# Whole-head scores in PSUM for the attention's softmax, and the pool mixer's window sums moved behind the state recurrence

## The chip, the cores and the metric

The kernel runs on one core of a Trainium2 chip. The metric is the device time of one execution in microseconds (us), taken as the median of several runs. TensorE (PE) does matmuls and writes to PSUM, VectorE (DVE) and ScalarE (ACT) read PSUM and do elementwise work and reductions, GpSimd (POOL) works in SBUF alone, and SyncE (SP) issues most transfers. Each engine runs its own instructions in order; engines wait for each other through semaphores.

## The reference, cut to what matters

Two transformer-like blocks follow each other on 1024 tokens of width 1024. The first has a bidirectional state-space mixer beside an attention, then a mixture of experts; the second has a pool mixer beside a state-space mixer, then a gated feed-forward network. The change touches two pieces.

```python
# first block, attention: 16 query heads on 4 key heads, 64 wide, 1024 queries, 256 + 1024 keys
s = jnp.einsum('bqhgd,bkhd->bhgqk', q_blk, k) * scale
pr = jax.nn.softmax(s, axis=-1)
o = jnp.einsum('bhgqk,bkhd->bqhgd', pr, v)
...
# second block: u = rmsnorm(h) @ w_in, one half to each mixer
for gi, w in enumerate((2, 4, 8, 16)):            # pool mixer, 128 channels per window
    mean = (c - lagged) / jnp.minimum(n_pos, float(w))
    diffs.append(mean - ug[:, :, gi])
y_pool = einsum('blgc,gcd->blgd', stack(diffs), w_pool) * pool_scale
...
y = gelu(state-space output)                      # state-space mixer: recurrence, then a gate
y = y * jax.nn.sigmoid(y @ w_glu + b_glu)
h = h + concatenate([y_pool, y_ssm]) @ w_out
```

## The kernel before

Products of fp32 values are made from a high and a low part, so a matrix product in `mm3` (lines 213 to 217) is three matmuls, and many tensors are split into a cast (ACT) and the rest (DVE or POOL).

**Attention** (`attention`, from line 1099). For each of 8 blocks of 128 queries and each of 4 key heads there is a group of 4 query heads, so 32 groups. A group's heads come as two pairs, and the work of a pair is cut into five *products* of at most 512 score columns: a head has T = 1280 of them (`PIECES`). The body of the loop over `s` (lines 1231 to 1246) is one *step*. It issues, in this order: `products(n)`, which are two accumulated matmuls of 512 columns, or four of 256 in the middle step of a pair; `maxima` of an earlier product on DVE; the `transposes` of the probabilities of four heads for one of the ten blocks of 128 keys (four matmuls into `pt`); `low`, the low part of an earlier transposed block (DVE); `exps`, the exponentials of a product (ACT), whose bias is the negated maximum and which add up their row sums; `norms`, the reciprocal of a sum (DVE) and the scaling of the probabilities (POOL); `high`, the cast of the transposed block (ACT); and `values`, two matmuls with the values into `pv`. At the end of a group `evacuate` copies `pv` out in two halves (ACT, lines 1223 and 1224) and POOL adds them. This order is written out by hand (`manual_schedule`), products run AHEAD = 17 steps before the values that use them.

Each product has a score tile of its own, one PSUM bank `S0` to `S4` with one buffer, so a bank is free for its next product five steps later, when its exponentials have read it. `pt` has two buffers and `pv` one. A head's maximum is made of three partial ones (`mx`), its sum of three partial sums on POOL (lines 1174 and 1175). The probabilities of a head stand in two tiles, `P0` (512 columns) and `P1` (768).

**Mixers of the second block** (`mixers`, from line 2115). TensorE projects while DVE runs the recurrence of states (`step`, `starts`, `combine`, lines 2199 to 2232), which fills `E`. Then come `out_ssm(q)` for four quarters (products with `E`, gelu on ACT), `turned(c)` (transposes, copies and a split of the gelu's output, its low part on DVE in line 2317), and the gate: eight products of twelve matmuls, each with a tanh (ACT) and a multiplication (DVE, line 2345). The generator `windows()` yields pieces of the window sums (DVE, lines 2253 to 2278): six are taken ahead of the gate, and the others two by two between its products; `pool_out(g)` (six matmuls, two evacuations on ACT) follows at three places between them and once at the end. The order on PE, DVE and POOL is written out by hand here too; ACT is left to the scheduler. The next stage (`out2`) multiplies all channels `yc` with `w_out`.

Of the kernel before, what the change touches and what calls it, by code (L numbers as in the profile page):

```python
# [10 lines left out]
F = mybir.dt.float32  # L11
# [154 lines left out]
class Kernel:  # L166
# [936 lines left out]
    def attention(self):  # L1103
# [6 lines left out]
        with es:  # L1110
# [6 lines left out]
            PIECES = (((0, 0, 512),), ((0, 512, 1024),), ((0, 1024, 1280), (1, 1024, 1280)), ((1, 0, 512),), ((1, 512, 1024),))  # L1117
            AHEAD = 17
            NG = 4 * NB
            P, split, pvs, bank = {}, {}, {}, {}  # L1120
            mx, neg, tot, rt = {}, {}, {}, {}

            def products(n):
# [7 lines left out]
                S = bank[n] = pp.tile([128, 512], F, name=f"S{k}")  # L1131
                o = 0
                for e, a, z in PIECES[k]:
                    for m in range(2):
                        nc.tensor.matmul(S[:, o:o + z - a], qS[b][:, 4 * j + 2 * p + e, :], kS[4 * m + j][:, a:z], start=m == 0, stop=m == 1)  # L1135
                    o += z - a

            def maxima(n):
                pair, k = divmod(n, 5)
                if n < 0 or pair >= 2 * NG:  # L1140
                    return
                if k == 0:
                    mx[pair] = wp.tile([128, 2, 3], F, name="mx")
                m = mx[pair]
                if k == 2:
                    V.tensor_reduce(m[:, :, 2], bank[n].rearrange("p (e n) -> p e n", e=2), axis=AX.X, op=OP.max)
                else:
                    V.tensor_reduce(m[:, k // 3, k % 3:k % 3 + 1], bank[n], axis=AX.X, op=OP.max)  # L1148
                if k in (2, 4):
                    e = k // 2 - 1  # L1150
                    h = 2 * pair + e

                    hd = wp.tile([128, 8], F, name="hd", bufs=6)
                    neg[h], tot[h], rt[h] = hd[:, 0:1], hd[:, 1:4], hd[:, 4:6]
                    V.tensor_reduce(neg[h], m[:, e, :], axis=AX.X, op=OP.max, negate=True)  # L1155

            def exps(n):

                pair, k = divmod(n, 5)
                if n < 0 or pair >= 2 * NG:  # L1160
                    return
                o = 0
                for e, a, z in PIECES[k]:
                    h = 2 * pair + e
                    half = int(a > 0)
                    if (h, half) not in P:
                        P[h, half] = wp.tile([128, 768 if half else 512], F, name=f"P{half}", bufs=9 if half else 6)
                    i = k - 2 * e
                    x = P[h, half][:, a - 512 * half:z - 512 * half]
                    nc.scalar.activation(x, bank[n][:, o:o + z - a], AF.Exp, bias=neg[h], accum_out=tot[h][:, i:i + 1])  # L1170
                    o += z - a
                    if k == 2 + 2 * e:
                        r = rt[h]
                        nc.gpsimd.tensor_add(r[:, 0:1], tot[h][:, 0:1], tot[h][:, 1:2])
                        nc.gpsimd.tensor_add(r[:, 1:2], r[:, 0:1], tot[h][:, 2:3])

            def norms(n):
                pair, k = divmod(n, 5)
                if n < 0 or pair >= 2 * NG or k not in (2, 4):
                    return  # L1180
                h = 2 * pair + k // 2 - 1
                r = rt[h]
                V.reciprocal(r[:, 0:1], r[:, 1:2])  # L1183
                for half in range(2):
                    nc.gpsimd.tensor_scalar(P[h, half], P[h, half], r[:, 0:1], 1.0, op0=OP.mult, op1=OP.mult)  # L1185
# [1526 lines left out]
```

## Time and profile before

| what | value |
|---|---|
| median of 3 runs (lowest, highest) | 2743.65 us (2742.18, 2745.04) |
| the profiled execution's own time | 2740.33 us |
| its span, first to last instruction | 2738.4 us |
| busy: PE, DVE, ACT, POOL | 2536.7 (93%), 1951.2 (71%), 1336.1 (49%), 976.5 (36%) us |
| mean granted TensorE clock | 0.959 of full speed |
| chain that ended last, by engine | PE 64%, DVE 16%, ACT 7%, DMA 6%, issue 5%, POOL 2% |
| attention, first to last score product | 800.3 to 1267.9 us |
| pool windows, their first and last shared additions (line 2264) | 1927.6 to 1952.6 us |

The page gives shares over the whole span, but the program is a row of stages with limits of their own. What a change of one stage is worth is read from that stage: from the busy time of its engines in windows of time, from what each engine waited for there, and from the timeline, where each row has a start, a duration and, in brackets, the idle time just before it and what ended it. A merged row ("x2") shows the time from the first start to the last end, and ends of matmuls are modelled, so the distance between starts tells more than their durations. The clock column says what share of the full 2.4 GHz TensorE was granted.

### The profile page before, as it was taken

The numbers are of one execution on the slowest core, as the hardware profiler recorded it, in microseconds if no ns is written. First come the engines' busy times: TensorE is split into PE (matmuls) and PEld (weight loads), VectorE is DVE, ScalarE is ACT, GpSimd is POOL, SyncE is SP. The second block draws the span as 40 slices with busy tenths as digits, with TensorE's granted clock in tenths as the row PEclk, the third lists the DMA queues.
The fourth block names the chain that finished last, engine by engine and source line by source line (L and its number), as shares of the span: only waits on it lengthen the run. The fifth ranks groups of instructions, "written<-read, shape, count | busy, mean of one in ns | idle before, by whom it ended". The sixth has DMA issues, their size and how long they took to land.

```text
span 2738.4 us, 36247 instructions
## 1 busy us (share of the span) xinstructions
PE 2536.7 (93%) x12369; PEld 2000.4 (73%) x12369; DVE 1951.2 (71%) x3735; ACT 1336.1 (49%) x2788; POOL 976.5 (36%) x1128
## 2 busy tenths in 40 slices
PE   7899999998899999998997999689799999999898
PEld 4676778854677777776775777577577788887787
DVE  7655676689649898897566777675647878775755
ACT  3233453456529999998223455343444333333433
POOL 5612011166016666666334455100241345443000
PEclk9999999988999999999987999899899999999999
DMA  7556421000610000002317788631312445547653
GB/s 270 175 189 204 155 71 39 32 8 1 245 62 17 17 17 32 17 1 69 116 70 221 223 263 264 215 109 46 112 54 74 164 148 184 173 159 269 232 196 116
DMA packets 141113, 344.21 MB, mean 126 GB/s; under 512 B 21200, under 2 KB 41344, under 8 KB 132064
## 3 DMA queue, kind: packets, MB, share of 16 engines
q1 hardware_dynamic: 88752, 198.03, 21.0%
q0 software_dynamic: 24176, 102.39, 11.5%
q10 hardware_dynamic: 28000, 41.46, 4.4%
q8 instruction: 98, 1.61, 0.2%
q14 instruction: 87, 0.71, 0.1%
HBM read 257.64 MB, written 93.62 MB: 128 GB/s over the span
## 4 chain that ended last, share of the span: by engine, by line
PE 64%; DVE 16%; ACT 7%; DMA 6%; issue 5%; POOL 2%; SPq 0%; ACTq 0%; DVEq 0%; POOLq 0%
PE m L217 5%; PE mm L215 5%; PE m L215 5%; PE m L216 5%; PE mm L217 5%; PE mm L216 5%; PE S L1135 5%; PE pt L1194 4%; PE a L216 3%; PE a L217 3%; PE a L215 2%; ACT P L1170 2%; PE pv L1215 2%; PE pv L1216 2%; PE cv L216 2%
## 5 line engine op out<-in xcount | busy, mean ns | idle before, releaser
L1203 DVE TENSOR_TENSOR pl<-pt,ph 128x512 fp32r<-128x512 f32 x320 | 219.1, 685 | 51.7 <-ACT ph L1199 46.3
L1170 ACT ACTIVATE P<-S,hd 128x512 f32<-128x512 f32 (+1 forms) x384 | 238.0, 624 | 1.8 <-DVE hd L1155 1.8
L1185 POOL TENSOR_SCALAR P<-P,hd 128x512 f32<-128x512 f32 (+1 forms) x256 | 202.7, 805 | 90.1 <-DVE hd L1183 85.5
L1135 PE MATMUL S<-kS,qS 128*128 128x512 f32 (+1 forms) x768 | 210.9, 372 | 19.1 <-ACT P L1170 19.1
L1199 ACT CAST ph<-pt 128x512 fp32r<-128x512 f32 x320 | 187.7, 587 | 28.0 <-PE pt L1194 14.5
L1194 PE MATMUL pt<-consts,P 128*128 128x128 f32 x1280 | 193.5, 273 | 6.0 <-DVE pl L1203 4.9
L1194 PEld LDWEIGHTS pt<-consts,P 128*128 128x128 f32 x1280 | 156.6, 140 | 45.2 <-DVE pl L1203 8.9
L1148 DVE TENSOR_REDUCE mx<-S 128x1 f32<-128x512 f32 x256 | 173.6, 679 | 3.0 <-PE S L1135 2.2
L1135 PEld LDWEIGHTS S<-kS,qS 128*128 128x128 f32 x768 | 128.3, 190 | 63.9 <-ACT P L1170 42.9
L1215 PE MATMUL pv<-ph,vS 128*128 128x512 f32 x320 | 151.3, 473 | 0.9 <-ACT ph L1199 0.3
L600 DVE SCALAR_TENSOR_TENSOR acc<-cv,vcol,acc 128x254 f32<-128x254 f32 (+5 forms) x288 | 110.3, 432 | 51.6 <-ACT acc L602 49.2
L2632 ACT CAST oh<-st 128x1024 fp32r<-128x1024 f32 x77 | 80.5, 1053 | 109.8 <-PE a L217 41.9
L216 PE MATMUL a<-ol,oh 128*128 128x512 f32 x308 | 122.0, 396 | 10.9 <-DVE ol L2633 10.9
L2633 DVE TENSOR_TENSOR ol<-st,oh 128x1024 fp32r<-128x1024 f32 x77 | 93.4, 1235 | 52.0 <-ACT oh L2632 45.1
L1216 PE MATMUL pv<-pl,vS 128*128 128x512 f32 x320 | 126.8, 396 | 0.2 <-DVE pl L1203 0.2
L217 PE MATMUL a<-oh,ol 128*128 128x512 f32 x308 | 121.7, 395 | 0.0
L215 PE MATMUL a<-oh 128*128 128x512 f32 x308 | 117.3, 391 | 0.3 <-DVE u L2550 0.3
L2440 ACT CAST gh<-gst 128x512 fp32r<-128x512 f32 x88 | 54.6, 621 | 128.1 <-PE m L216 122.0
L216 PE MATMUL mm<-wl,hH 128*128 128x512 f32 x288 | 114.6, 398 | 2.2 <-DVE wl L255 2.0
L215 PE MATMUL mm<-wh,hH 128*128 128x512 f32 x288 | 115.4, 401 | 0.0
L217 PE MATMUL mm<-wh,hL 128*128 128x512 f32 x288 | 113.5, 394 | 0.0
L217 PE MATMUL cv<-hH,wl 128*128 128x512 f32 (+1 forms) x288 | 104.0, 361 | 1.0 <-POOL wl L584 1.0
(785 smaller groups left out, 7494.5 us busy)
## 6 DMA issues: line engine op xcount, KB each, us to landing
gst<-in_ffn_gu_dram SPq DMA_DIRECT2D x88, 256.0 KB, 3.3
st<-hop SPq DMA_DIRECT2D x77, 256.0 KB, 7.4
wmod<-in_w_mod_dram ACTq DMA_DIRECT2D x64, 256.0 KB, 4.0
hop<-h POOLq DMA_DIRECT2D x44, 256.0 KB, 2.6
d<-in_ffn_down_dram SPq DMA_DIRECT2D x22, 512.0 KB, 3.5
wop<-d POOLq DMA_DIRECT2D x22, 512.0 KB, 3.5
st<-wop SPq DMA_DIRECT2D x44, 256.0 KB, 5.0
wst<-in_w_in_dram SPq DMA_DIRECT2D x40, 256.0 KB, 3.6
```

The source lines that it names most:

```text
L215: nc.tensor.matmul(out, lh, rh, start=first, stop=False)
L216: nc.tensor.matmul(out, lh, rl, start=False, stop=False)
L217: nc.tensor.matmul(out, ll, rh, start=False, stop=last)
L1135: nc.tensor.matmul(S[:, o:o + z - a], qS[b][:, 4 * j + 2 * p + e, :], kS[4 * m + j][:, a:z], start=m == 0, stop=m == 1)
L1148: V.tensor_reduce(m[:, k // 3, k % 3:k % 3 + 1], bank[n], axis=AX.X, op=OP.max)
L1170: nc.scalar.activation(x, bank[n][:, o:o + z - a], AF.Exp, bias=neg[h], accum_out=tot[h][:, i:i + 1])
L1185: nc.gpsimd.tensor_scalar(P[h, half], P[h, half], r[:, 0:1], 1.0, op0=OP.mult, op1=OP.mult)
L1194: nc.tensor.transpose(pt[:, i, :], P[4 * g + i, int(c > 3)][:, o:o + 128], self.ident)
L1199: nc.scalar.copy(split[n][1], split[n][0])
L1203: V.tensor_sub(split[n][2], split[n][0], split[n][1])
L1215: nc.tensor.matmul(pv, v, ph, start=c == 0, stop=False)
L1216: nc.tensor.matmul(pv, v, pl, start=False, stop=c == NBT - 1)
```

## The change

In the attention the five score tiles become one tile `S` of two whole heads, 2 x 1280 columns without a gap, over five banks; the middle bank holds the end of the first head and the start of the second. The pieces of the second head are cut anew (0 to 256, 256 to 768, 768 to 1280). A head gets one maximum, one exponential with one sum, one reciprocal and one scaling, all over 1280 columns, once its last product is issued (`head(n)` says when). The partial maxima, the POOL additions of sums and the two-part probabilities go. The exponentials stand two steps behind the products where it was four, the norms three where it was five, and AHEAD is 16. In the mixer, `window(3 - q)` is no generator any more and is issued whole, behind `out_ssm(q)`; `pool_out` follows one quarter later, `turned(0)` as before behind the third quarter, and the gate's loop holds nothing else.

```diff
@@ -1114,11 +1114,11 @@
             vS = cp.tile([128, NBT, 512], R, name="vS")
             nc.sync.dma_start(vS[:].bitcast(F), self.vv[:].rearrange("b p n -> p b n").bitcast(F))
 
-            PIECES = (((0, 0, 512),), ((0, 512, 1024),), ((0, 1024, 1280), (1, 1024, 1280)), ((1, 0, 512),), ((1, 512, 1024),))
-            AHEAD = 17
+            PIECES = (((0, 0, 512),), ((0, 512, 1024),), ((0, 1024, 1280), (1, 0, 256)), ((1, 256, 768),), ((1, 768, 1280),))
+            S = pp.tile([128, 2, T], F, name="S")
+            AHEAD = 16
             NG = 4 * NB
-            P, split, pvs, bank = {}, {}, {}, {}
-            mx, neg, tot, rt = {}, {}, {}, {}
+            P, split, pvs, cols = {}, {}, {}, {}
 
             def products(n):
 
@@ -1128,70 +1128,41 @@
                     return
                 if n % 40 == 30 and b + 1 < NB:
                     self.load_q(b + 1)
-                S = bank[n] = pp.tile([128, 512], F, name=f"S{k}")
-                o = 0
                 for e, a, z in PIECES[k]:
                     for m in range(2):
-                        nc.tensor.matmul(S[:, o:o + z - a], qS[b][:, 4 * j + 2 * p + e, :], kS[4 * m + j][:, a:z], start=m == 0, stop=m == 1)
-                    o += z - a
+                        nc.tensor.matmul(S[:, e, a:z], qS[b][:, 4 * j + 2 * p + e, :], kS[4 * m + j][:, a:z], start=m == 0, stop=m == 1)
+
+            def head(n):
+
+                pair, k = divmod(n, 5)
+                return None if n < 0 or pair >= 2 * NG or k not in (2, 4) else 2 * pair + k // 2 - 1
 
             def maxima(n):
-                pair, k = divmod(n, 5)
-                if n < 0 or pair >= 2 * NG:
-                    return
-                if k == 0:
-                    mx[pair] = wp.tile([128, 2, 3], F, name="mx")
-                m = mx[pair]
-                if k == 2:
-                    V.tensor_reduce(m[:, :, 2], bank[n].rearrange("p (e n) -> p e n", e=2), axis=AX.X, op=OP.max)
-                else:
-                    V.tensor_reduce(m[:, k // 3, k % 3:k % 3 + 1], bank[n], axis=AX.X, op=OP.max)
-                if k in (2, 4):
-                    e = k // 2 - 1
-                    h = 2 * pair + e
-
-                    hd = wp.tile([128, 8], F, name="hd", bufs=6)
-                    neg[h], tot[h], rt[h] = hd[:, 0:1], hd[:, 1:4], hd[:, 4:6]
-                    V.tensor_reduce(neg[h], m[:, e, :], axis=AX.X, op=OP.max, negate=True)
+                h = head(n)
+                if h is not None:
+
+                    cols[h] = wp.tile([128, 8], F, name="hd", bufs=6)
+                    V.tensor_reduce(cols[h][:, 0:1], S[:, h % 2], axis=AX.X, op=OP.max, negate=True)
 
             def exps(n):
-
-                pair, k = divmod(n, 5)
-                if n < 0 or pair >= 2 * NG:
-                    return
-                o = 0
-                for e, a, z in PIECES[k]:
-                    h = 2 * pair + e
-                    half = int(a > 0)
-                    if (h, half) not in P:
-                        P[h, half] = wp.tile([128, 768 if half else 512], F, name=f"P{half}", bufs=9 if half else 6)
-                    i = k - 2 * e
-                    x = P[h, half][:, a - 512 * half:z - 512 * half]
-                    nc.scalar.activation(x, bank[n][:, o:o + z - a], AF.Exp, bias=neg[h], accum_out=tot[h][:, i:i + 1])
-                    o += z - a
-                    if k == 2 + 2 * e:
-                        r = rt[h]
-                        nc.gpsimd.tensor_add(r[:, 0:1], tot[h][:, 0:1], tot[h][:, 1:2])
-                        nc.gpsimd.tensor_add(r[:, 1:2], r[:, 0:1], tot[h][:, 2:3])
+                h = head(n)
+                if h is not None:
+                    P[h] = wp.tile([128, T], F, name="P", bufs=8)
+                    nc.scalar.activation(P[h], S[:, h % 2], AF.Exp, bias=cols[h][:, 0:1], accum_out=cols[h][:, 1:2])
 
             def norms(n):
-                pair, k = divmod(n, 5)
-                if n < 0 or pair >= 2 * NG or k not in (2, 4):
-                    return
-                h = 2 * pair + k // 2 - 1
-                r = rt[h]
-                V.reciprocal(r[:, 0:1], r[:, 1:2])
-                for half in range(2):
-                    nc.gpsimd.tensor_scalar(P[h, half], P[h, half], r[:, 0:1], 1.0, op0=OP.mult, op1=OP.mult)
+                h = head(n)
+                if h is not None:
+                    V.reciprocal(cols[h][:, 2:3], cols[h][:, 1:2])
+                    nc.gpsimd.tensor_scalar(P[h], P[h], cols[h][:, 2:3], 1.0, op0=OP.mult, op1=OP.mult)
 
             def transposes(n):
                 g, c = divmod(n, NBT)
                 if n < 0 or g >= NG:
                     return
                 pt = pp.tile([128, 4, 128], F, name="pt", bufs=2)
-                o = 128 * (c - 4 if c > 3 else c)
                 for i in range(4):
-                    nc.tensor.transpose(pt[:, i, :], P[4 * g + i, int(c > 3)][:, o:o + 128], self.ident)
+                    nc.tensor.transpose(pt[:, i, :], P[4 * g + i][:, 128 * c:128 * c + 128], self.ident)
                 split[n] = pt, wp.tile([128, 4, 128], R, name="ph", bufs=4), wp.tile([128, 4, 128], R, name="pl", bufs=4)
 
             def high(n):
@@ -1236,10 +1207,10 @@
                     maxima(n - 1)
                     transposes(s + 2)
                     low(s + 1)
-                    exps(n - 4)
+                    exps(n - 2)
                     if last:
                         evacuate(s)
-                    norms(n - 5)
+                    norms(n - 3)
                     high(s + 2)
                     if not last:
                         values(s)
@@ -2266,24 +2237,17 @@
                         V.tensor_add(nx[:, 17:], u[:, 1:], u[:, 0:L - 1])
                         V.tensor_copy(nx[:, 16:17], u[:, 0:1])
                     cur = nx
-                    yield
                 t16 = pw.tile([128, 16], F, name="t16")
                 V.tensor_mul(t16, cur[:, 16:32], rc[:, 16 * g:16 * g + 16])
                 d = cur[:, 16:]
                 V.scalar_tensor_tensor(d, d, 1.0 / (2 << g), u, op0=OP.mult, op1=OP.subtract)
                 V.tensor_sub(d[:, 0:16], t16, u[:, 0:16])
-                yield
                 dh, dl = pw.tile([128, L], R, name="dh"), pw.tile([128, L], R, name="dl")
                 nc.scalar.copy(dh, d)
                 V.tensor_sub(dl, d, dh)
                 outs[g] = dh, dl
-                yield
 
             outs = {}
-
-            def windows():
-                for g in (3, 2, 1, 0):
-                    yield from window(g)
 
             def pool_out(g):
                 dh, dl = outs[g]
@@ -2322,16 +2286,17 @@
             V.tensor_scalar(hb, vc[:, off["b_glu"][0]:off["b_glu"][0] + 4], 0.5, None, op0=OP.mult)
             for q in range(4):
                 out_ssm(q)
-                if q > 1:
-                    turned(q - 2)
+                window(3 - q)
                 if q == 2:
-                    V.tensor_sub(wgl, wg, wgh)
+                    turned(0)
+                if q:
+                    pool_out(4 - q)
+            V.tensor_sub(wgl, wg, wgh)
+            turned(1)
+            pool_out(0)
             turned(2)
             turned(3)
             self.dump("Y", Y)
-            win = windows()
-            for _ in range(6):
-                next(win)
             for c in range(4):
                 for n in range(2):
                     s = slice(512 * n, 512 * n + 512)
@@ -2343,14 +2308,6 @@
                     nc.scalar.activation(th, ps, AF.Tanh, bias=hb[:, c:c + 1])
                     y = self.yc[:, 4 + c, s]
                     V.scalar_tensor_tensor(y, th, 1.0, y, op0=OP.add, op1=OP.mult)
-                    if c or n:
-                        for _ in range(2):
-                            next(win, None)
-                    if (c, n) in ((1, 1), (2, 1), (3, 1)):
-                        pool_out(4 - c)
-            for _ in win:
-                pass
-            pool_out(0)
             man.close()
             self.dump("yc", self.yc)
         s_es.close()
```

The built program shows what that makes of each engine's instructions; a bracket names the semaphores (by engine) that an instruction waits for.

TensorE in the attention before, from the last matmul of one product over three steps (`S_7989` and the like are the banks of their products; further transposes of a step are left out):

```order
L1135 MATMUL S_7989<-kS_6346,qS 128x512
L1194 MATMUL pt<-consts,P_7664 128x128 [waits DVE_49]
L1215 MATMUL pv<-ph,vS 128x512
L1216 MATMUL pv<-pl,vS 128x512
L1135 MATMUL S_8010<-kS_6342,qS 128x256 [waits Activation_49]
L1135 MATMUL S_8010<-kS_6346,qS 128x256
L1194 MATMUL pt<-consts,P_7664 128x128 [waits DVE_49]
L1215 MATMUL pv<-ph,vS 128x512
L1216 MATMUL pv<-pl,vS 128x512
L1135 MATMUL S_8032<-kS_6342,qS 128x512 [waits Activation_49]
L1135 MATMUL S_8032<-kS_6346,qS 128x512
```

and with the change, over as much of the program, from the fourth product of a pair (`S` is the one tile; `kS_6343` and the like are keys of key heads; behind the first step the transposes and values are left out):

```order
L1133 MATMUL S<-kS_6343,qS 128x512
L1133 MATMUL S<-kS_6347,qS 128x512
L1165 MATMUL pt<-consts,P 128x128 [waits DVE_49]
L1186 MATMUL pv<-ph,vS 128x512 [waits Activation_49]
L1187 MATMUL pv<-pl,vS 128x512
L1133 MATMUL S<-kS_6343,qS 128x512 [waits DVE_49]
L1133 MATMUL S<-kS_6347,qS 128x512
L1133 MATMUL S<-kS_6344,qS 128x512 [waits Activation_49]
L1133 MATMUL S<-kS_6348,qS 128x512
L1133 MATMUL S<-kS_6344,qS 128x512 [waits DVE_49]
L1133 MATMUL S<-kS_6348,qS 128x512
L1133 MATMUL S<-kS_6344,qS 128x256 [waits Activation_49]
```

Before, each product waits for ACT. Now the fourth product of a pair waits for nothing, the fifth for DVE, and in the next pair the first for ACT, the second for DVE and the third, of 256 columns, for ACT.

DVE in the attention before, some three steps:

```order
L1146 TENSOR_REDUCE mx<-S_8118 128x2 [waits PE_49]
L1155 TENSOR_REDUCE hd<-mx 128x1 [waits DVE_49]
L1203 TENSOR_TENSOR pl<-pt,ph 128x512 [waits Activation_49]
L1148 TENSOR_REDUCE mx<-S_8141 128x1 [waits PE_49]
L1203 TENSOR_TENSOR pl<-pt,ph 128x512 [waits Activation_49]
L1183 RECIPROCAL hd<-hd 128x1 [waits Pool_49]
L1148 TENSOR_REDUCE mx<-S_8161 128x1 [waits PE_49]
L1155 TENSOR_REDUCE hd<-mx 128x1 [waits DVE_49]
```

and with the change, from one reciprocal over one pair of heads:

```order
L1156 RECIPROCAL hd<-hd 128x1
L1145 TENSOR_REDUCE hd<-S 128x1 [waits PE_49,Pool_49]
L1174 TENSOR_TENSOR pl<-pt,ph 128x512 [waits DVE_49,Activation_49]
L1174 TENSOR_TENSOR pl<-pt,ph 128x512 [waits Activation_49]
L1145 TENSOR_REDUCE hd<-S 128x1 [waits PE_49,Activation_49,Pool_49]
L1174 TENSOR_TENSOR pl<-pt,ph 128x512 [waits DVE_49,Activation_49]
L1156 RECIPROCAL hd<-hd 128x1
```

Five reductions of a pair became two over the whole tile. The first head's waits for PE and POOL, the second head's also for ACT.

DVE in the mixer before, from the last addition of the recurrence (`E`) to the first window sums (`pn`):

```order
L2232 TENSOR_TENSOR E<-E,p 128x4x120
L2322 TENSOR_SCALAR hb_18924<-vcol 128x4 [waits PE_49]
L2317 TENSOR_TENSOR yl<-yc,yh 128x1024 [waits PE_49,Activation_49]
L2328 TENSOR_TENSOR wgl<-wg,wgh 128x2048 [waits DMAHW1_49]
L2317 TENSOR_TENSOR yl<-yc,yh 128x1024 [waits Activation_49] x3
L2262 MEMSET pn 128x16 [waits DMAHW3_49]
L2266 TENSOR_TENSOR pn<-yc 128x1023
L2267 COPY pn<-yc 128x1
L2262 MEMSET pn 128x16
L2264 TENSOR_TENSOR pn<-pn 128x1024 [waits DVE_49]
```

and with the change:

```order
L2203 TENSOR_TENSOR E<-E,p 128x4x120
L2286 TENSOR_SCALAR hb_17454<-vcol 128x4 [waits PE_49]
L2233 MEMSET pn 128x16 [waits DMAHW3_49]
L2237 TENSOR_TENSOR pn<-yc 128x1023 [waits Activation_49]
L2238 COPY pn<-yc 128x1
L2233 MEMSET pn 128x16
L2235 TENSOR_TENSOR pn<-pn 128x1024 [waits DVE_49]
```

The window sums stood behind the four low parts `yl` of the gate's inputs and the split of its weights (`wgl`), and now stand right behind the recurrence.

## Rows read from the trace of the kernel before

**Rows 1.** Windows of the attention; us, busy us (instructions) by engine, clock, DMA.

```profile
1000.00:1050.00 50.00, 48.67 (x287) 39.38 (x286) 45.25 (x95) 47.06 (x124) 30.97 (x62) 1.00 0.07 22
```

**Rows 2.** Groups by shape, 860 to 1240 us: busy us, mean ns, idle before.

```profile
L1203 DVE TENSOR_TENSOR pl<-pt,ph 128x512 fp32r<-128x512 f32 x256 | 175.4, 685 | 35.5 <-ACT ph L1199 31.1
...
L1199 ACT CAST ph<-pt 128x512 fp32r<-128x512 f32 x256 | 150.0, 586 | 21.2 <-PE pt L1194 9.9
L1170 ACT ACTIVATE P<-S,hd 128x512 f32<-128x512 f32 x205 | 142.7, 696 | 0.0
L1148 DVE TENSOR_REDUCE mx<-S 128x1 f32<-128x512 f32 x205 | 139.2, 679 | 0.7
...
L1170 ACT ACTIVATION_READ_ACCUMULATOR P<-S,hd 128x1 f32 x306 | 62.9, 205 | 0.0
...
L1170 ACT ACTIVATE P<-S,hd 128x256 f32<-128x256 f32 x102 | 47.7, 478 | 0.0
```

**Rows 3.** Waits, 860 to 1240 us: us in total, times, longest.

```profile
PEld S L1135 <- ACT P L1170: 28.7, 51, 0.9
PE S L1135 <- ACT P L1170: 11.0, 26, 0.4
```

**Rows 4.** Line 1223, the copies that start a group's evacuation: ns, first and last start.

```profile
L1223 ACT COPY lo<-pv x32: 582/583/584, 833.1 to 1294.2; 64x512 f32<-64x512 f32 x32
```

**Rows 5.** Timeline of TensorE in the attention: start us, us, what, idle before.

```profile
1037.09 0.64 PE L1135 MATMUL S<-kS,qS 128*128 128x512 f32 x2
1037.56 0.60 PE L1194 MATMUL pt<-consts,P 128*128 128x128 f32 x4
1037.92 0.48 PE L1215 MATMUL pv<-ph,vS 128*128 128x512 f32 x1
1038.23 0.39 PE L1216 MATMUL pv<-pl,vS 128*128 128x512 f32 x1
1038.46 0.62 PE L1135 MATMUL S<-kS,qS 128*128 128x512 f32 x2
...
1041.18 0.74 PE L1135 MATMUL S<-kS,qS 128*128 128x256 f32 x4
1041.76 0.60 PE L1194 MATMUL pt<-consts,P 128*128 128x128 f32 x4
...
1043.54 0.73 PE L1135 MATMUL S<-kS,qS 128*128 128x512 f32 x2 [0.42 <-ACT P L1170]
```

**Rows 6.** Waits in the mixer, 1860 to 2000 us.

```profile
PE mm L215 <- ACT dh L2277: 7.5, 3, 3.5
...
PE mm L216 <- DVE dl L2278: 2.1, 3, 0.8
```

**Rows 7.** Groups by shape in the mixer, 1790 to 2010 us.

```profile
L2295 ACT ACTIVATE yc<-mm,vcol 128x512 f32<-128x512 f32 x8 | 5.5, 691 | 6.6 <-PE mm L217 6.5
...
L2278 DVE TENSOR_TENSOR dl<-pn,dh 128x1024 fp32r<-128x1024 f32 x4 | 4.9, 1225 | 3.0 <-ACT dh L2277 3.0
...
L2277 ACT CAST dh<-pn 128x1024 fp32r<-128x1024 f32 x4 | 4.2, 1044 | 4.2 <-DVE pn L2274 4.2
```

**Rows 8.** Timeline of ACT in the attention: one exponential.

```profile
1042.71 0.69 ACT L1170 ACTIVATE P<-S,hd 128x512 f32<-128x512 f32 x1
1043.29 0.20 ACT L1170 ACTIVATION_READ_ACCUMULATOR P<-S,hd 128x1 f32 x1
```

**Rows 9.** Timeline of TensorE in the mixer, where the granted clock is low.

```profile
1927.20 0.63 PE L217 MATMUL mm<-yh,wgl 128*128 128x512 f32 x1
1927.62 0.63 PE L215 MATMUL mm<-yh,wgh 128*128 128x512 f32 x1
```

**Rows 10.** Windows of the mixer, columns as in rows 1.

```profile
1960.00:1970.00 10.00, 5.05 (x10) 3.20 (x11) 6.23 (x9) 5.49 (x9) 0.00 (x0) 0.66 0.51 187
```

**Rows 11.** Windows of the attention's start.

```profile
812.00:814.00 2.00, 1.42 (x7) 0.86 (x7) 1.74 (x4) 1.71 (x7) 1.90 (x4) 1.00 0.00 0
...
818.00:820.00 2.00, 1.30 (x11) 1.06 (x10) 1.58 (x3) 2.00 (x7) 0.51 (x3) 1.00 0.00 0
```

## The prediction, made before the changed kernel was run

> **What bounds the kernel now.** I read the windows first. In the attention's steady stretch TensorE is busy 48.67 of every 50 us at the full clock [rows 1]. ACT with 47.06 and DVE with 45.25 are close behind, POOL with 30.97 is not, so the stage ends with TensorE, and two engines have little to give. The groups by shape [rows 2] carry the prices of one reduction, exponential, cast and subtraction. The waits show what TensorE still loses: in 380 us it waits 28.7 us (weight load) and 11.0 us (matmul) for ACT's exponentials, and for DVE it is not listed as waiting [rows 3]. The period comes from the 32 evacuations of one group of four heads: 833.1 to 1294.2 us over 31 intervals, 14.87 us each [rows 4]. One group is two pairs of heads, ten steps; **a pair takes 7.44 us now.** The timeline of TensorE shows one step [rows 5]: products at 1037.09, transposes at 1037.56, values at 1037.92, next products at 1038.46. That is 1.37 us, 0.47 for the products and 0.90 for what follows. The step with four short matmuls takes 0.58 for them (1041.18 to 1041.76). A pair without waits would be 4 x 1.37 + 1.48 = 6.96, so waits cost 0.48 per pair, 31 us in 64 pairs. This is what the attention half of the change could win at most.
>
> In the mixer, by the waits from 1860 to 2000 us, TensorE stands 7.5 us for the high parts of the pool windows and 2.1 us for the low parts [rows 6].
>
> **The change, part by part.**
>
> *Attention, instructions.* Per pair it removes five reductions and two small ones, six exponentials and four POOL additions, and puts two reductions and two exponentials over 1280 in their place; four POOL multiplications become two. DVE, ACT and POOL all do less, and no queue gets a new transfer. By itself that is worth nothing beyond the waits, since TensorE does the same matmuls.
>
> *Attention, waits.* This is the term that decides. The five score tiles, each a bank with its own life, become one tile S. The order rows above show what that does: the product of a pair's fifth step waits for DVE, that of the next pair's first step for ACT, of its second for DVE, of its third for ACT; only the fourth follows freely. Before, each product waited for ACT alone, for the exponential of its own bank five products earlier. By the counts that these waits hold in the built program the releaser is always the youngest access to S, also where it lies in other banks. The first head's reduction (products 1 to 3) is held until the *fourth* product has ended, the fifth product until that reduction has ended, the exponential until the fifth product, the next pair's first product until that exponential, the second head's reduction until that product, and so on. Products, reductions and exponentials form **one chain**, in which nothing that touches S overlaps.
>
> Its links, from rows:
> - Reduction over 1280: 512 take 0.679 [rows 2]; DVE's slope is 1.225 at 1024 [rows 7] less 0.685 at 512 [rows 2], 1.05 ns an element, so 0.68 + 0.81 = 1.49 us.
> - Exponential: 0.478 at 256, 0.696 at 512 [rows 2], 0.218 per 256, so 1.35 at 1280. The read of its sum starts 0.11 before that end and takes 0.20 (1043.29 against 1042.71 + 0.69), and the next product starts 0.05 after it, at 1043.54 [rows 5, 8]. So it holds S for 1.44.
> - A product that starts from a wait: 0.73 (1043.54); one that doesn't: 0.64 (1037.09) [rows 5].
> - A hop between engines: 0.05, as from 1043.49 to 1043.54.
>
> One round for a pair: two reductions 2.98, two exponentials 2.88, three products after waits 2.19, the third step from its products to the next ones 0.58 + 0.90 = 1.48, the fourth product 0.64, eight hops 0.40. Together **10.57 us against 7.44**. Transposes and values (0.90) run inside the 1.5 us links, so they hide, as do the casts on ACT and subtractions on DVE: five of each with the long instructions make under 7 us of work per engine and pair. What comes late next is a subtraction that queues behind a long reduction on DVE and holds the next transposes; it falls into the same gaps. 64 x 3.13 = **+200 us**. Bounds: products at 0.64 throughout and hops near 0.04 give 10.2 (+177); transposes that wait 0.1 more in three links give 10.9 (+221).
>
> *Start of the attention.* In the first three pairs there are no transposes, and TensorE works 0.47 of each 2.2 us. Matmuls on the low clock start 0.42 apart [rows 9] against 0.23 [rows 5], 0.38 more per product; some 13 products, **+5 us**, between 0 and 8.
>
> *Pool mixer.* The windows move from between the gate's products to behind the recurrence, where DVE has little to do while the scans' outputs are computed. The 9.6 us of waits [rows 6] can go, and part of the low clock behind them (0.66 from 1960 to 1970 [rows 10]), say 3 us. On the other side ACT gets pool evacuations of 0.691 and a high part of 1.044 [rows 7] into the stretch where it turns the gate's inputs, and the gate's last inputs come later: four evacuations and one high part, 3.8 us, plus one more queueing. Sum **-7 us**; bounds -12.6 (nothing given back) and 0. The DVE subtraction for the gate weights, moved behind the windows, and DMA order are costed at nothing: the gate's first product starts after both.
>
> *Sum.* +200 + 5 - 7 = +198 us. Against the profiled execution, 2738.4 in the trace and 2740.33 in all, that is 2938; the median of the runs shown is 3.3 us higher, 2743.65, so the forecast is **2942 us**.
>
> **The rivals.**
>
> *Waits by bank.* If a product could run beside a reduction of other banks, only the exponentials would hold TensorE. ACT is free for the exponential 0.27 into its step: transposes end at 1038.16, the cast (0.586, of which 0.11 overlaps) 0.57 later, and the step starts at 1038.46 [rows 2, 5]. Then 1.44 + 0.05 gives 1.76, against a step of 1.37: 0.39 per head, so 6.96 + 0.78 = 7.74 per pair, +19 us, and 2756 in all. For it: the banks are disjoint. Against it: the order rows show a product waiting for DVE twice per pair, and no release of a disjoint bank needs that. The Trainium skill (PSUM — Partial Sum Buffer, Summary: rules for kernel authors) advises guarding by bank and reading one bank while the matmul writes another; a schedule by that rule is this rival, and no run here shows it yet.
>
> *Faster.* If the reductions and exponentials, now fewer, were always done before TensorE arrives, the attention would run at 6.96 per pair: -31 - 7, so 2706. It decides at the point where a reduction with its hop fits beside transposes and values; that is 1.54 against 0.90, so it fails by a wide margin unless the waits mean an older instruction than I read. That the change then does just what its words say, and no more, speaks for it.
>
> *The clock falls.* With TensorE at two thirds, the granted clock could drop to 1.2 GHz for stretches. Five products then cost 0.38 more each, and transposes and values, at 1.8, stick out of four links by 0.3 and lengthen the third step by 0.9: 4.0 us per pair, +256 for the whole stage and +128 for half of it, 3070. Against it: from 812 to 820 us TensorE was busy 1.42 and 1.30 of 2 us, with gaps in every group, and the clock stayed at 1.00 [rows 11]. The Trainium skill (TensorE: Matmul & The Clock Gate, A second HAM failure mode: psum-queue depth-cycling) reports a kernel whose short idles between matmul groups made the clock swing; by that rule this rival is the outcome, and the stretch from 812 us disagrees at nearly the same load.
>
> **Chances.** The chain as summed 0.87; the falling clock 0.07; waits by bank 0.03; faster 0.02; no effect 0.01. A difference of 0.2%, 5.5 us, is about what a measurement of this kernel can tell from no change. Faster is 0.02, same 0.01, slower 0.97, as the bank rival is 12 us slower too. The bounds of the three terms give 2743.65 + 177 - 12.6, or 2908, to 2743.65 + 221 + 8, or 2973. I take 2900 to 2975 and leave out most of the clock rival.
>
> **What would show it.** Right: evacuations about 21 us apart; per pair two waits of TensorE for the reduction near 0.8 us and two for the exponential near 0.7; TensorE at about two thirds, full clock; reductions of 1.49 and exponentials of 1.35; ACT, DVE and POOL all less busy than now; no wait of the pool products in the mixer, and the output product 5 to 10 us sooner after the recurrence. Wrong: products that start while a reduction is running, an evacuation period under 16 us, or a granted clock under 0.9 in the steady stretch.

## The result and the profile after

The changed kernel takes **2952.4 us** (median of 4 runs, 2947.18 to 2958.63) against 2744.35 (2742.18 to 2751.96) for the kernel before in the same comparison: a ratio of 1.076 with a 95% interval of 1.0741 to 1.0778. The profiled execution took 2952.1 us, its span is 2950.3. The same code stands on lower lines in the changed kernel: 2 lower in the products, 29 lower from the transposes to the experts, 31 and more in the mixer.

The page's first part, and a window of the steady attention as in [rows 1]:

```profile
PE 2598.6 (88%) x12369; PEld 1979.0 (67%) x12369; DVE 1915.3 (65%) x3415; ACT 1276.4 (43%) x2276; POOL 897.5 (30%) x744
```

```profile
1100.00:1150.00 50.00, 38.47 (x198) 25.57 (x197) 28.28 (x42) 28.60 (x48) 15.47 (x14) 1.00 0.06 22
```

No engine is full any more: DVE went from 45.25 to 28.28 of 50 us, ACT from 47.06 to 28.60, and TensorE from 48.67 to 38.47, at a granted clock of 1.00. When every engine has room and the stage is slower, look for a chain. The waits from 880 to 1400 us (us in total, times, longest) have rows that [rows 3] did not: TensorE waits for DVE, once per head, 0.9 us on average.

```profile
ACT P L1151 <- PE S L1133: 126.4, 98, 1.7
PEld S L1133 <- DVE hd L1145: 123.0, 97, 1.6
...
DVE hd L1145 <- PE S L1133: 117.4, 72, 2.0
...
PE S L1133 <- DVE hd L1145: 85.7, 97, 1.2
PEld S L1133 <- ACT P L1151: 76.5, 98, 0.9
```

TensorE waits for DVE and for ACT, DVE for TensorE, ACT for TensorE: a circle. The timeline shows it turning once, from one second head's reduction to the next (start us, us, what, idle before):

```profile
1101.69 1.49 DVE L1145 TENSOR_REDUCE hd<-S 128x1 f32<-128x1280 f32 x1 [1.97 <-PE S L1133]
...
1103.23 0.73 PE L1133 MATMUL S<-kS,qS 128*128 128x512 f32 x2 [0.78 <-DVE hd L1145]
1104.00 1.33 ACT L1151 ACTIVATE P<-S,hd 128x1280 f32<-128x1280 f32 x1 [1.34 <-PE S L1133]
...
1105.47 0.74 PE L1133 MATMUL S<-kS,qS 128*128 128x256 f32 x4 [0.46 <-ACT P L1151]
...
1106.96 0.62 PE L1133 MATMUL S<-kS,qS 128*128 128x512 f32 x2
1107.69 1.49 DVE L1145 TENSOR_REDUCE hd<-S 128x1 f32<-128x1280 f32 x1 [1.00 <-PE pt L1165]
...
1109.23 0.74 PE L1133 MATMUL S<-kS,qS 128*128 128x512 f32 x2 [0.75 <-DVE hd L1145]
1110.01 1.33 ACT L1151 ACTIVATE P<-S,hd 128x1280 f32<-128x1280 f32 x1 [1.37 <-PE S L1133]
...
1111.48 0.73 PE L1133 MATMUL S<-kS,qS 128*128 128x512 f32 x2
1112.34 1.49 DVE L1145 TENSOR_REDUCE hd<-S 128x1 f32<-128x1280 f32 x1 [1.97 <-PE S L1133]
```

No two of these overlap beyond the modelled ends of matmuls, and the round takes 10.65 us. Over the whole stage, the copies that answer to [rows 4]:

```profile
L1194 ACT COPY lo<-pv x32: 582/582/584, 855.9 to 1510.3; 64x512 f32<-64x512 f32 x32
```

31 intervals of 21.11 us against 14.87.

**Where 212 us of span went.** Attention, from its first product to the last such copy: 709.0 us against 493.9, +215.1 (it also began 1.0 later). From there to the last addition into `E`: 601.4 against 590.1, +11.3. From that addition to the first output product: 72.5 against 83.9, -11.4. From there to the end: -4.1. Together +211.9.

### The profile page after: what moved, and what is told of

It is laid out like the page before. It is cut to its first block, busy times and chain, and to the rows that moved or that the text cites. A ratio compares the mean times of both kernels' runs of the same rounds, so it can differ in the third digit from the quotient of the medians.

```text
span 2950.3 us, 35366 instructions
## 1 busy us (share of the span) xinstructions
PE 2598.6 (88%) x12369; PEld 1979.0 (67%) x12369; DVE 1915.3 (65%) x3415; ACT 1276.4 (43%) x2276; POOL 897.5 (30%) x744
## 4 chain that ended last, share of the span: by engine, by line
PE 59%; DVE 20%; DMA 7%; ACT 6%; issue 6%; POOL 2%; DVEq 0%; SPq 0%; POOLq 0%; ACTq 0%
PE S L1133 8%; DVE hd L1145 6%; PE mm L215 5%; PE mm L216 5%; PE mm L217 5%; PE m L217 4%; PE m L215 4%; PE m L216 4%; ACT P L1151 3%; PE a L216 2%; PE a L217 2%; PE a L215 2%; PE pt L1165 2%; PE cv L217 2%; PE cv L216 2%
## 5 line engine op out<-in xcount | busy, mean ns | idle before, releaser
L1133 PE MATMUL S<-kS,qS 128*128 128x512 f32 (+1 forms) x768 | 233.4, 401 | 165.7 <-DVE hd L1145 116.0
L1145 DVE TENSOR_REDUCE hd<-S 128x1 f32<-128x1280 f32 x128 | 190.9, 1491 | 199.5 <-PE S L1133 165.7
L1133 PEld LDWEIGHTS S<-kS,qS 128*128 128x128 f32 x768 | 118.5, 194 | 277.1 <-DVE hd L1145 166.2
L1157 POOL TENSOR_SCALAR P<-P,hd 128x1280 f32<-128x1280 f32 x128 | 171.1, 1336 | 422.7 <-DVE hd L1156 416.7
L1174 DVE TENSOR_TENSOR pl<-pt,ph 128x512 fp32r<-128x512 f32 x320 | 211.8, 681 | 98.0 <-ACT ph L1170 98.0
L1151 ACT ACTIVATE P<-S,hd 128x1280 f32<-128x1280 f32 x128 | 170.0, 1328 | 176.9 <-PE S L1133 176.3
L1165 PEld LDWEIGHTS pt<-consts,P 128*128 128x128 f32 x1280 | 149.4, 142 | 68.2 <-issue 45.4
```

The lines of the kernel that those rows point to most:

```text
L1133: nc.tensor.matmul(S[:, e, a:z], qS[b][:, 4 * j + 2 * p + e, :], kS[4 * m + j][:, a:z], start=m == 0, stop=m == 1)
L1145: V.tensor_reduce(cols[h][:, 0:1], S[:, h % 2], axis=AX.X, op=OP.max, negate=True)
L1151: nc.scalar.activation(P[h], S[:, h % 2], AF.Exp, bias=cols[h][:, 0:1], accum_out=cols[h][:, 1:2])
L1157: nc.gpsimd.tensor_scalar(P[h], P[h], cols[h][:, 2:3], 1.0, op0=OP.mult, op1=OP.mult)
L1165: nc.tensor.transpose(pt[:, i, :], P[4 * g + i][:, 128 * c:128 * c + 128], self.ident)
L1174: V.tensor_sub(split[n][2], split[n][0], split[n][1])
```

## The experiments

Nine kernels ran, each beside the kernel before; a ratio is to the runs of that one in the same comparison (medians 2741.0 to 2747.0 us). *Group* is the distance of the copies above in the steady stretch; *mixer* runs from the start of the last addition into `E` to the first output product.

| kernel | median, us | ratio to before (95%) | group | mixer |
|---|---|---|---|---|
| before | 2744.35 | | 14.85 | 83.9 |
| changed | 2952.4 | 1.0741 to 1.0778 | 21.3 | 72.5 |
| e_pool | 2729.4 | 0.9939 to 0.9971 | 14.85 | 74.4 |
| e_attn | 2963.2 | 1.0780 to 1.0844 | 21.3 | 85.3 |
| e_threetile | 2736.7 | 0.9965 to 1.0003 | 14.90 | 72.7 |
| e_best | 2718.5 | 0.9894 to 0.9942 | 14.38 | 74.3 |
| e_onetile | 3051.3 | 1.1083 to 1.1144 | 24.11 | 85.5 |
| e_twomax | 3238.0 | 1.1761 to 1.1827 | 30.7 | 73.2 |
| e_extra512 | 3026.1 | 1.1015 to 1.1077 | 23.83 | 72.6 |
| e_late | 2716.4 | 0.9877 to 0.9911 | 14.38 | 73.5 |
| e_split | 2713.7 | 0.9889 to 0.9927 | 14.38 | 69.9 |

### The two halves apart: e_pool, e_attn

e_pool has the attention of before with the changed mixer, e_attn the reverse. (e_pool against the changed kernel.)

```diff
-            S = pp.tile([128, 2, T], F, name="S")
-            AHEAD = 16
...
+            AHEAD = 17
...
+                S = bank[n] = pp.tile([128, 512], F, name=f"S{k}")
```

> The pool mixer's half of the change alone: the attention is the one of before, the window sums stand right behind the recurrence. If the halves add up: from the end of the recurrence to the first output product 72 us as in the changed kernel, against 83 before, and the kernel at 2744 - 11 = 2733 us (2729 to 2737). Rival, what the mixer wins is given back behind it: 2744 (2741 to 2746).

> The attention's half alone: one tile S of two heads, the pool windows between the gate's products as before. If the halves add up: attention of 709 us from the first product to the last evacuation against 494, and 2952 + 11 = 2963 us (2958 to 2970). Rival, the halves interact, for example through transfers of the experts that start later: 2952 or less.

2729.4 and 2963.2, both inside their ranges: the halves add up, -13.0 and +220.8 against +208.1 for the whole. (From the end of the recurrence e_pool's mixer took 73.7 us, where 72 were expected.) The changed kernel's mixer alone is a gain of 0.3 to 0.6%, its attention alone a loss of 8%.

### The tile's identity alone: e_onetile

```diff
             AHEAD = 17
+            SS = pp.tile([128, 5, 512], F, name="S")
...
-                S = bank[n] = pp.tile([128, 512], F, name=f"S{k}")
+                S = bank[n] = SS[:, k, :]
```

> The kernel before with one edit: its five score tiles are five slices of one tile of five banks; no instruction changes its size, its columns or its place, and no two products share a bank. Theory, that a wait on a tile is for its youngest access, whatever the bank: per product one chain of 0.78 (product and hop), 0.73 (reduction and hop) and 0.84 (exponential, its sum and hop), 12.1 us per pair for 7.43, some 300 us more: 3042 us (2990 to 3080). Rival, waits by bank, so that the changed kernel's chain comes from the middle bank which two heads share there: 2744 (2735 to 2755).

3051.3 us, 12.05 us per pair where 12.1 were expected. The copies of a group, the waits from 900 to 1300 us, and one turn of the circle:

```profile
L1224 ACT COPY lo<-pv x32: 582/582/586, 871.5 to 1604.6; 64x512 f32<-64x512 f32 x32
```

```profile
PEld S L1136 <- ACT P L1171: 178.5, 150, 1.6
DVE mx L1149 <- PE S L1136: 136.6, 133, 1.5
ACT P L1171 <- DVE mx L1149: 129.8, 116, 1.3
PE S L1136 <- ACT P L1171: 116.5, 149, 1.4
```

```profile
1016.19 0.74 PE L1136 MATMUL S<-kS,qS 128*128 128x256 f32 x4 [1.40 <-ACT P L1171]
...
1016.97 0.69 DVE L1149 TENSOR_REDUCE mx<-S 128x1 f32<-128x512 f32 x1 [1.29 <-PE S L1136]
...
1017.72 0.69 ACT L1171 ACTIVATE P<-S,hd 128x512 f32<-128x512 f32 x1
...
1018.54 0.73 PE L1136 MATMUL S<-kS,qS 128*128 128x512 f32 x2 [0.43 <-ACT P L1171]
```

The reduction at 1016.97 is over the product of the step before, in another bank (`maxima(n - 1)`), and yet it starts only behind the product of 1016.19.

The same instructions on the same number of banks, named as one tile, cost 300 us. So neither long instructions nor the shared middle bank are needed for the loss: the waits follow the tile. The *waits by bank* rival is out. (The one tile is also taken once, ahead of the loop, where before each product took a new one. No run takes a tile of five banks anew for each pair, so which of the two makes the waits so coarse is open.) The rule of the Trainium skill beside that rival (PSUM — Partial Sum Buffer, Summary: rules for kernel authors) asks for guards by bank; this run does not contradict it as advice, it shows that one tile over five banks is guarded more coarsely here.

### The long instructions without the one tile: e_threetile

```diff
-            S = pp.tile([128, 2, T], F, name="S")
+            S, mx = {}, {}
...
+                if k in (0, 2, 3):
+                    S[pair, (k + 1) // 2] = pp.tile([128, 512 if k == 2 else 1024], F, name=f"S{(k + 1) // 2}")
...
+                    V.tensor_reduce(m[:, k // 4, 0:1], S[pair, k // 2], axis=AX.X, op=OP.max)
...
+                        V.tensor_reduce(m[:, :, 1], S[pair, 1].rearrange("p (e n) -> p e n", e=2), axis=AX.X, op=OP.max)
```

> The changed kernel, with its five banks as three tiles (1024 columns of the first head, the two ends of 256, 1024 columns of the second head) in place of one; reductions over 1024 and 512, exponentials over 1024 and 256, at the same steps as in the changed kernel. Theory, that what costs the time is the chain through one tile, not the long instructions: a product then waits for an exponential of its own tile alone, a group takes 14.9 to 15.4 us as it did before (14.85), and with the mixer's gain the kernel takes 2733 to 2750 us, say 2741. Rival, that long reductions and exponentials delay TensorE by themselves, as they stand in front of casts and subtractions: a group stays above 18 us, and the kernel above 2840.

(The pieces are again those of before.) 2736.7 us, a group of 14.90. Groups by shape, 880 to 1200 us:

```profile
L1136 PE MATMUL S<-kS,qS 128*128 128x512 f32 x343 | 109.9, 401 | 0.0
L1149 DVE TENSOR_REDUCE mx<-S 128x1 f32<-128x1024 f32 x86 | 104.5, 1215 | 0.0
...
L1164 ACT ACTIVATE P<-S,hd 128x1024 f32<-128x1024 f32 x86 | 95.9, 1115 | 0.0
```

Reductions of 1.22 and exponentials of 1.12 us, four fifths of a head in one piece, and the 512-column products wait 0.0 us. The chain is the cause, and long instructions by themselves cost little: 0.05 us per group. (e_pool, with the same mixer, is 7 us faster by the medians; 3.2 us of difference lie in the attention by the traces.)

### A longer link: e_twomax, e_extra512

```diff
 V.tensor_reduce(cols[h][:, 0:1], S[:, h % 2], axis=AX.X, op=OP.max, negate=True)
+V.tensor_reduce(cols[h][:, 0:1], S[:, h % 2], axis=AX.X, op=OP.max, negate=True)
```

> The changed kernel with each head's reduction over 1280 columns issued twice in a row, the second writing the same value again. Theory of one chain: each adds its 1.49 us and a hop of about 0.03 to the chain, 128 times: 195 us more, 2952 + 195 = 3147 us (3120 to 3165), and a group takes 27.3 us for 21.3. Rival, that DVE has room in the stretch (57% busy) and the second one hides beside other links: under 3000.

3238.0 us, far above the expectation: 286 us more than the changed kernel where 195 were expected. Windows, DVE and TensorE of this run:

```profile
1000.00:1050.00 50.00, 33.46 (x138) 23.76 (x136) 31.70 (x37) 18.62 (x31) 9.43 (x8) 0.80 0.06 21
1050.00:1100.00 50.00, 34.88 (x136) 25.26 (x134) 27.84 (x34) 20.33 (x34) 10.85 (x10) 0.74 0.00 0
```

```profile
999.99 1.49 DVE L1145 TENSOR_REDUCE hd<-S 128x1 f32<-128x1280 f32 x1 [2.38 <-PE S L1133]
1001.51 1.49 DVE L1146 TENSOR_REDUCE hd<-S 128x1 f32<-128x1280 f32 x1
```

```profile
1003.06 1.22 PE L1133 MATMUL S<-kS,qS 128*128 128x512 f32 x2 [2.27 <-DVE hd L1146]
1004.08 1.05 PE L1166 MATMUL pt<-consts,P 128*128 128x128 f32 x4
```

The duplicate adds its 1.52 us to the chain as expected (999.99 to 1001.51). The rest is the clock: TensorE now stands still for 2.3 us at each reduction, the granted clock alternates between its two levels and averages 0.74 to 0.80, and the pair of matmuls at 1003.06 takes 1.22 us for the 0.73 at full clock. By the starts in the trace a round is 4.69 us longer than the changed kernel's 10.65: 3.04 in the two reductions, and 1.65 in the links that are TensorE's work. What the prediction's *falling clock* rival describes happens here, but not in the changed kernel. The swing that the Trainium skill reports for short idles between matmul groups (TensorE: Matmul & The Clock Gate, A second HAM failure mode: psum-queue depth-cycling) is in this trace (0.74 to 0.80), and not in that of the changed kernel (1.00). So a step between the two was tried, with a shorter addition:

```diff
+V.tensor_reduce(cols[h][:, 6:7], S[:, h % 2, 0:512], axis=AX.X, op=OP.max)
 V.tensor_reduce(cols[h][:, 0:1], S[:, h % 2], axis=AX.X, op=OP.max, negate=True)
```

> The changed kernel with one more reduction per head, over the head's first 512 columns, into a column that nothing reads, just ahead of the one over 1280. Theory of one chain at the full clock: 0.60 to 0.71 us more in each of 128 links, 77 to 91 us: 3035 us (3025 to 3048), and a group of 23.7 to 24.2 us for 21.3, with a granted clock of 1.00 in the stretch. Rival, waits of 1.5 us are already enough for the clock to fall, as waits of 2.3 us were in the run with the doubled reduction: the clock under 0.95 and over 3055.

3026.1 us, inside the expected range, and a group of 23.83, inside too; the 74 us above the changed kernel are a little less than the 77 to 91 expected.

```profile
1100.00:1200.00 100.00, 67.81 (x348) 44.70 (x346) 62.47 (x93) 51.27 (x85) 29.84 (x27) 1.00 0.03 11
```

```profile
1085.00 0.73 PE L1133 MATMUL S<-kS,qS 128*128 128x512 f32 x2 [1.36 <-DVE hd L1146]
```

Here TensorE waits 1.36 us at a reduction and the clock stays at 1.00. (23.83 - 21.31) / 4 = 0.63 us per link for a reduction that holds DVE 0.61: what a link gains, the kernel loses.

### A version that beats both: e_best, e_late, e_split

```diff
-            AHEAD = 16
+            EXPS = {4: ['A0'], 0: ['M0'], 1: ['M1', 'B1']}
+            NORMS = {1: 0, 3: 1}
+            AHEAD = 18
...
-                    P[h] = wp.tile([128, T], F, name="P", bufs=8)
+                    P[h, i] = wp.tile([128, 256 if i else 1024], F, name=f"P{i}", bufs=8 if i else 8)
```

(e_best against e_threetile. Keys of `EXPS` are the steps of a pair; A and B are the 1024 columns of the first and second head, M the 256 of each.)

> Three tiles as in the run before it, with the exponentials spread over three steps (first head's 1024, then its 256, then the second head's two), probabilities in two tiles, and AHEAD 18, so that the copies of pv stand in a step without an exponential. Theory: DVE and ACT each save two fixed costs per pair, products no longer wait, a group takes 14.4 to 14.7 us against 14.85: 5 to 14 us less in the attention, and with the mixer's 11 us 2722 (2716 to 2731). Rival, that DVE, busy 90% of the stretch, now holds TensorE through the subtractions: a group of 14.9 to 15.3, and 2735 to 2748.

2718.5 us, a group of 14.38.

```profile
1000.00:1050.00 50.00, 49.97 (x293) 39.16 (x292) 45.41 (x84) 43.70 (x97) 28.55 (x49) 1.00 0.06 22
```

TensorE is busy 49.97 of 50 us, where it was 48.67 [rows 1]. With the score tiles apart, a kernel of fewer and longer softmax instructions does win, 0.47 us per group; the attention takes 481.2 us from its first product to the last copy, against 493.9. But e_threetile, with reductions and exponentials of the same sizes, won nothing: the gain came only with the new places of the exponentials and AHEAD 18. Whether these would also help the short instructions of before was not tried.

Two more runs took up TensorE's waits in the mixer. (Their expectations count to the first output product with a low part, 1.0 to 1.1 us behind the moment of the table.)

```diff
                 if q == 2:
                     turned(0)
+                    V.tensor_sub(wgl, wg, wgh)
...
-            V.tensor_sub(wgl, wg, wgh)
             turned(1)
-            pool_out(0)
...
+                    if (c, n) == (0, 1):
+                        pool_out(0)
```

> The kernel of three tiles and AHEAD 18 with two more edits in the mixer: the last window's pool products behind the gate's second product, and the split of the gate's weights ahead of the last window. Theory: of the 8.8 us that TensorE still waits between the recurrence and the first output product, the 4.6 us for the last window's high and low part go, because ACT casts it 5 us late and TensorE then has other work; the first output product comes 71 us after the recurrence for 75, and the kernel takes 2714 us (2709 to 2719). Rival, the gate's inputs are late by the same amount, and the waits only move to them: 75 us and 2718 (2714 to 2724).

The rival held: 73.5 us for 74.3, though the median, 2716.4, lies in both ranges. DVE, then TensorE, of e_late:

```profile
1915.85 1.23 DVE L2272 TENSOR_TENSOR dl<-pn,dh 128x1024 fp32r<-128x1024 f32 x1 [7.07 <-ACT dh L2271]
1916.99 1.22 DVE L2306 TENSOR_TENSOR yl<-yc,yh 128x1024 fp32r<-128x1024 f32 x1
```

```profile
1918.27 0.80 PE L216 MATMUL mm<-yl,wgh 128*128 128x512 f32 x1 [5.57 <-DVE yl L2306]
```

Nobody needed `dl` now, but it stood first in DVE's queue, so the gate's low parts behind it were late. e_split takes it out of their way:

```diff
+                outs[g] = d
+                if g:
+                    parts(g)
+
+            def parts(g):
+                d = outs[g]
                 dh, dl = pw.tile([128, L], R, name="dh"), pw.tile([128, L], R, name="dl")
...
             turned(3)
+            parts(0)
```

> The kernel of the run with the last pool products in the gate, with one more edit: the last window's cast and subtraction are issued behind the gate's last inputs, and no longer ahead of them. Theory: there DVE's subtraction for the last window waited 7.1 us for ACT's cast, and three finished inputs of the gate stood behind it in DVE's queue, which TensorE then waited for (5.6 us); with the subtraction behind them, TensorE's waits between the recurrence and the first output product shrink from 9.7 us to 4 to 6, the first output product comes 69 to 71 us after the recurrence for 74.6, and the kernel takes 2712 us (2707 to 2716). Rival, ACT's copies for the gate's inputs set that moment anyway: 74 us, 2716 (2713 to 2720).

The mixer falls to 69.9 us (71.0 to the product that the expectation counts to), TensorE's waits in it to 5.2 (e_late's were 8.7, not the 9.7 written there), and the median to 2713.7. By total time e_best, e_late and e_split can't be told apart, their intervals overlap; the trace tells e_split's mixer from the others. e_split is 1% faster than the kernel before.

## Why the prediction was right, point by point

- **The chain, +200.** Right, by the mechanism named; a little small. The links, predicted and measured on the timeline above: reduction with hop 1.54, 1.54; product to exponential 0.78, 0.77 and 0.78; exponential to product 1.49, 1.47; third step 1.48, 1.49; fourth product to reduction 0.69, 0.73; next pair's first product to the second reduction 0.78, 0.86. Round 10.57, measured 10.65. The pair before, in the steady stretch, was 7.42 rather than 7.44, so the term is 64 x 3.23 = 207. That transposes, values, casts and subtractions hide in the links held: the round is made up of the links alone.
- **Start of the attention, +5.** A little small, with a part left out. By the starts of the pairs, the second to fourth took 12.0, 12.0 and 13.0 us for the steady 10.65, 5.0 us more, as priced for the low clock. Not in the term: before, with no transposes yet, the first three pairs took 6.3, 4.7 and 4.6 us for the steady 7.42, 6.7 less, while the changed kernel saved only 4.1, in its first pair (6.5). Together that is some 7.5, just inside the bound of 8, and 215.1 less 207 leaves under 1 for the end. The prediction let the low clock last three pairs; it lasted from 806 to 840 us, into the first transposes (windows of the changed kernel; the kernel before had 1.00 from 810 on):

```profile
811.00:821.00 10.00, 5.40 (x12) 2.55 (x11) 1.66 (x2) 2.84 (x4) 2.54 (x2) 0.50 0.03 10
821.00:831.00 10.00, 5.25 (x15) 3.23 (x14) 3.22 (x4) 2.08 (x3) 2.66 (x2) 0.50 0.00 0
831.00:841.00 10.00, 8.55 (x30) 6.52 (x30) 3.51 (x6) 4.30 (x8) 2.66 (x2) 0.53 0.00 0
```

- **Pool mixer, -7.** Right in sign and inside the bounds, too small: -11.4 in the trace. (Over all traces the mixer of before took 83.9 to 85.5 us, the changed one 72.5 to 74.4.) Of 9.6 us of waits [rows 6], 4.6 came back, for the last window alone, since ACT casts it late (below); with the waits for the gate's inputs and for the output, TensorE's waits in this stretch fell from 14.6 to 8.9 us. Of the other 5.7 us, about 1.9 are ten small matmuls that TensorE had already done when the last addition into `E` began (308 matmuls fall into the stretch, 318 before). The rest goes with a better clock (on average 0.93 for 0.91) and is near the 3 us that the prediction took. It does not end there: the ten microseconds from the first output product had a clock of 0.73 before and have 1.00 now, 2.7 of the last 4.1 us in the account above. TensorE's waits from 2111 to 2187 us:

```profile
PE mm L215 <- ACT dh L2246: 4.1, 1, 4.1
PE mm L216 <- DVE yl L2281: 1.8, 2, 1.0
PE mm L215 <- ACT yh L2362: 1.3, 1, 1.3
PE mm L215 <- ACT yh L2280: 1.2, 2, 0.8
PE mm L216 <- DVE dl L2247: 0.5, 1, 0.5
```

- **Not in the sum.** The stretch from the attention to `E`, whose code is the same, took 11.3 us longer. It holds ACT's waits for the experts' weights, here before and then after:

```profile
ACT guh L1629 <- DMA wst<-in_moe_gate_dram,eid: 28.2, 10, 6.0
```

```profile
ACT guh L1600 <- DMA wst<-in_moe_gate_dram,eid: 34.0, 10, 6.2
```

  In e_pool, e_attn, e_best and e_threetile the same stretch took 589.9, 592.0, 592.6 and 596.5 us. e_attn has the long attention and no loss here, so it seems to follow the execution, and not the length of the attention; what sets it was not tried. No term covered this stretch. In the trace the sum is 14 us short (198 for 211.9): 7 in the chain and 11.3 here, less the 4.4 that the mixer won beyond its term; the other misses cancel, by luck.
- **The signs given.** Copies 21 us apart: 21.11. Two waits of TensorE per pair for the reduction near 0.8: 0.78 and 0.75. For the exponential near 0.7: less, 0.46, and one that only the weight load shows. TensorE at two thirds: the page's modelled busy time says 77%; counted by starts, the pair's 6.96 us of work are 65% of 10.65. Reductions 1.49, exponentials 1.33 for 1.35, full clock, and ACT, DVE and POOL all less busy. Two signs failed, both in the mixer: the pool products still wait (4.6 us), and the output product comes 11.4 us sooner, not 5 to 10.
- **The rivals.** *Faster* fell with the time itself and *waits by bank* with e_onetile; *the clock falls* was the right thing to fear, one step further along, as e_twomax shows.

## What to carry to other kernels

Merging tiles to save instructions also merges their lives: in the built program, look at which instruction each wait stands for, and where a tile is written, reduced and read by three engines in turn, add up one round of it as a chain, since no busy share will show it. Keep one tile for each life (here 1024 columns of a head), and take the longer instructions then. An instruction that waits in an in-order queue also delays finished work behind it, so issue what nobody is waiting for last.

## What the runs showed of the hardware that was not expected

With repeated waits of 0.9 us on average (changed kernel) and of 1.36 us (e_extra512) at a reduction, the granted clock read 1.00 in the steady stretch; with waits of 2.3 us (e_twomax) it read 0.74 to 0.80, and the run took 91 us on top of the chain's own. At the start, where the products come with nothing beside them, the clock stayed at 0.50 from 806 to 840 us. And a reduction took 0.68 us over 512 columns, 1.22 over 1024 (two banks, e_threetile) and 1.49 over 1280 (three banks): no step at the borders of banks.
